# Attention scores of a head pair: one head after the other, or both heads' passes in turn into two PSUM tiles

## The chip, the cores and the metric

The kernel runs on one core of one Trainium2 chip. The metric is device time in microseconds (us) of one execution. Before the change the median of three executions is 1733.63 us (1733.34 to 1735.73).

The core has engines that work side by side and wait for one another through semaphores: TensorE (PE in the profile, with its weight loads as PEld), VectorE (DVE), ScalarE (ACT), GpSimd (POOL) and SyncE (SP), which here issues the weight transfers. Data lie in SBUF, 128 partitions wide. TensorE writes into PSUM, which this kernel uses as eight banks of 128 x 512 fp32 values.

## The reference

A trunk of two layers over 256 latent and 256 context tokens, model width 1024. Layer 0 has a recurrent mixer, layer 1 windowed attention; each stands between two SwiGLU feed-forwards. The change lies in the attention of layer 1 (16 query heads of width 64, 4 key/value heads, blocks of 128 queries):

```python
s_band = jnp.where(valid, jnp.einsum('bqhgd,bkhd->bhgqk', qj, kj).astype(f32), -jnp.inf)
s_ctx = jnp.einsum('bqhgd,bkhd->bhgqk', qj, kc)
p_ctx, p_band = _softmax_with_sink(sink, s_ctx, s_band)
return (jnp.einsum('bhgqk,bkhd->bqhgd', p_ctx.astype(vc.dtype), vc)
        + jnp.einsum('bhgqk,bkhd->bqhgd', p_band.astype(vj.dtype), vj))
```

Each latent query sees 256 context keys and its window of latent keys; with 256 latent tokens that is 512 keys, of which one block of 128 is partly masked. The softmax also has a sink logit for each head.

## The kernel before

Activations are kept transposed (features on partitions, tokens along the row), and every product of the model is made from fp32 values split into a high and a low part in the fp32r type: high x high, high x low, low x high, three matmuls into one PSUM bank (lines 415 to 417; line 444 for the first four blocks of a stage, line 710 in the feed-forwards). SyncE streams the weights in transfers of up to 1 MB; ACT casts the high part (line 259), DVE subtracts for the low part (line 243).

In the attention stage (`odd`) the 16 query heads are packed in eight pairs T = 0 to 7. A pair's query tile `Q[T]` holds one head (half 0) on partitions 0 to 63 and the other (half 1) on 64 to 127; `Q[T][:, 0]` is the high part and `Q[T][:, 1]` the low one. The keys `KH` and `KL` lie the same way, so that each half is a matmul over 64 partitions: `psc` takes 128 queries by 512 keys. With two query blocks t there are four items per T, 32 in all. One item is:

- TensorE: three 64-row passes into one bank `psc` (line 1277 high x high, 1278 high x low, 1279 low x high), and a 128-row bf16 matmul that adds the mask to one block of 128 keys (line 1281, identity `IDB` as weights);
- DVE: the row maximum over `psc` (line 1283) and the scaled, negated bias (line 1284);
- ACT: the exponential into `P` with the row sum (line 1288), put off to the next step;
- four steps later (`LAG`): TensorE turns `P` into `ppt` (line 1298), ACT copies that to `PT` (line 1299).

The loop over n has one item per step. A step stands in this order: work put off by earlier steps (`self.sub`, `self.later`), scores of item n, at the second item of a T the rotary turn of the next pair's queries (`q_rope`: matmul `psw`, line 1224; DVE lines 1229 to 1231; ACT casts the high part, line 1243, DVE makes the low part, line 1244), one quarter of a query projection (`q_piece`, six matmuls of lines 415 to 417, for n up to 24 except n = 8), transposes of item n - 4, and at the first item of a T the values of pair T - 2 (`pov`, line 1313, and the row factors `prs`, line 1319; then lines 1322 to 1325). From n = 31 on the first matmuls of the output projection (line 444) are put between. Each engine works through its instructions in the order in which this code is written. PSUM tiles take the eight banks in turn, and one waits until the bank's earlier tile has been read. `P` has five buffers, `Q` three.

Of the kernel before, what the change touches and what calls it, by code (L numbers as in the profile page):

```python
# [12 lines left out]
AF = mybir.ActivationFunctionType  # L13
ALU = mybir.AluOpType
AX = mybir.AxisListType
# [131 lines left out]
class Trunk:  # L147
# [1054 lines left out]
    def odd(self):  # L1202
        nc, V, S, G, M = self.nc, self.V, self.S, self.G, self.M
        self.narrow()
        with self.tc.tile_pool(name="od", bufs=1) as op:
# [4 lines left out]
            KH = op.tile([128, 2, 512], F32R, name="KH")  # L1210
            KL = op.tile([128, 2, 512], F32R, name="KL")
# [5 lines left out]
            NSK = op.tile([128, 16], F32, name="NSK")  # L1217
            V.tensor_scalar(NSK, SK, -1.0, None, ALU.mult)

            Q, ST, PT, P = {}, {}, {}, {}  # L1220
# [18 lines left out]
            def q_rope(T, stage):  # L1239
                t = raws.pop(T)  # L1240
                rope(t, swap(t), t)
                q = Q[T] = op.tile([128, 2, 256], F32R, tag="q", name="q", bufs=3)
                stage(lambda: S.copy(q[:, 0], t),
                      lambda: V.tensor_tensor(q[:, 1], t, q[:, 0].bitcast(F32), ALU.subtract))

            def k_rope(i):
                x = KF[i][:, 256:512]
                rope(x, swap(x), x)
                self.later(lambda: S.copy(KH[:, i], KF[i]),
                           lambda: V.tensor_tensor(KL[:, i], KF[i], KH[:, i].bitcast(F32), ALU.subtract))  # L1250

            pss = self.split_start("o", 2)
# [3 lines left out]
            for T in range(2):  # L1256
                ps = self.bank()
# [7 lines left out]
            def head_of(T, half):  # L1265
                return (2 * (T // 4) + half) * 4 + T % 4

            def scores(T, half, t):
                g = 2 * (T // 4) + half
                if half == t == 0:  # L1270
                    ST[T] = op.tile([128, 5, 4], F32, tag="st", name="st", bufs=4)
                i = 2 * half + t
                st = ST[T]
                b = slice(64 * half, 64 * half + 64)
                ps = self.bank("psc")
                q = slice(128 * t, 128 * t + 128)
                M.matmul(ps, lhsT=Q[T][b, 0, q], rhs=KH[b, g // 2, :], start=True, stop=False, skip_group_check=True)  # L1277
                M.matmul(ps, lhsT=Q[T][b, 0, q], rhs=KL[b, g // 2, :], start=False, stop=False, skip_group_check=True)  # L1278
                M.matmul(ps, lhsT=Q[T][b, 1, q], rhs=KH[b, g // 2, :], start=False, stop=False, skip_group_check=True)  # L1279
                kt = 3 - t  # L1280
                M.matmul(ps[:, 128 * kt:128 * kt + 128], lhsT=self.IDB, rhs=self.MKB[:, 1 - t], start=False, stop=True, skip_group_check=True)
                hd = head_of(T, half)
                V.tensor_reduce(st[:, 0, i:i + 1], ps, AX.X, ALU.max)
                V.tensor_scalar(st[:, 1, i:i + 1], st[:, 0, i:i + 1], -0.125, NSK[:, hd:hd + 1], ALU.mult, ALU.min)

                def exp():
                    p = P[T, half, t] = op.tile([128, 512], F32, tag="P", name="P", bufs=5)
                    S.activation(p, ps, AF.Exp, scale=0.125, bias=st[:, 1, i:i + 1], accum_out=st[:, 2, i:i + 1])

                self.later(exp)  # L1290

            def transposes(T, half, t):
                if t == 0:
                    PT[T, half] = op.tile([128, 4, 256], F32, tag="PT", name="PT", bufs=4)
                p = P.pop((T, half, t))
                ps = self.bank("ppt")
                for k in range(4):
                    M.transpose(ps[:, 128 * k:128 * k + 128], p[:, 128 * k:128 * k + 128], self.ID)  # L1298
                S.copy(PT[T, half][:, :, 128 * t:128 * t + 128], ps.rearrange("p (k q) -> p k q", k=4))
                if half == t == 1:  # L1300
                    st = ST[T]
                    for x in range(2):
                        hd = head_of(T, x)
                        S.activation(st[:, 3, 2 * x:2 * x + 2], st[:, 1, 2 * x:2 * x + 2], AF.Exp, bias=SK[:, hd:hd + 1])
                    V.tensor_tensor(st[:, 2], st[:, 2], st[:, 3], ALU.add)
                    V.reciprocal(st[:, 4], st[:, 2])

            def values(T):
                ps = self.bank("pov")
                for kt in range(4):  # L1310
                    for half in range(2):
                        g = 2 * (T // 4) + half
                        M.matmul(ps[64 * half:64 * half + 64, 0:256], lhsT=VT[:, kt, 64 * g:64 * g + 64],  # L1313
                                 rhs=PT[T, half][:, kt, :], start=kt == 0, stop=kt == 3, skip_group_check=True)
                pr = self.bank("prs")
                for t in range(2):
                    for half in range(2):
                        i = 2 * half + t
                        M.matmul(pr[64 * half:64 * half + 64, 128 * t:128 * t + 128], lhsT=ST[T][:, 4, i:i + 1].to_broadcast([128, 64]),
                                 rhs=self.ID, start=True, stop=True)  # L1320
                rb = self.tmp("rb")
                S.copy(rb[:, 0:256], pr[:, 0:256])
                self.later(lambda: V.tensor_tensor(rb[:, 256:512], ps[:, 0:256], rb[:, 0:256], ALU.mult),
                           lambda: S.copy(OH[:, T], rb[:, 256:512]),
                           lambda: V.tensor_tensor(OL[:, T], rb[:, 256:512], OH[:, T].bitcast(F32), ALU.subtract))
                PT.pop((T, 0))
                PT.pop((T, 1))
                Q.pop(T)
                ST.pop(T)

            items = [(T, half, t) for T in range(8) for half in range(2) for t in range(2)]
            LAG = 4
            PIECES = {p + (p >= 8): p for p in range(24)}
            EARLY = range(31, 36)
# [2 lines left out]
            def q_piece(T, i):  # L1337
                if i == 0:
                    qp[T] = self.bank()
                wh, wl = self.weight(("oq", T))  # L1340
                for kt in (2 * i, 2 * i + 1):
                    c = slice(128 * kt, 128 * kt + 128)
                    self.mm3(qp[T][:, 0:256], wh[:, c], wl[:, c], self.NH[:, kt, 256:512], self.X[1][kt][:, 256:512], kt == 0, kt == KT - 1)
                if i == 3:
                    q_load(T, qp.pop(T))
                    self.done(("oq", T))

            for n in range(len(items) + LAG + 1):
                T, i = n // 4, n % 4
                self.sub()  # L1350
                if n < len(items):
                    scores(*items[n])
                if i == 1 and T < 7:
                    q_rope(T + 1, self.later)
                if n == 3:
                    k_rope(1)
                if n in PIECES:
                    p = PIECES[n]
                    q_piece(2 + p // 4, p % 4)
                if LAG <= n < len(items) + LAG:  # L1360
                    transposes(*items[n - LAG])
                if i == 0 and T > 1:
                    values(T - 2)
                if n == EARLY[0]:
                    pss = [self.bank() for _ in range(4)]
                    early = self.steps(pss, "oo", [(0, 256)] * 4, src=os)
                if n in EARLY:
                    next(early)
# [5 lines left out]
            for m in range(8):  # L1374
                ps = pss[m] if m < 4 else self.bank()
# [185 lines left out]
```

## Time and profile before

| | us |
|---|---|
| median of three executions | 1733.63 |
| span of the profiled execution, first to last instruction | 1731.2 |
| PE busy | 1719.7 |
| DVE busy | 1145.0 |
| ACT busy | 653.7 |
| score matmuls, lines 1277 to 1281, first to last start | 1418.5 to 1499.8 |

Of the profiled execution the record gives the span and no other time; the three executions that were timed lie 2.1 to 4.5 us above that span. The granted TensorE clock is 0.998 of full speed on average. Times within the profile are counted from the span's first instruction. A matmul's own duration runs from its start until its result is out; since matmuls are pipelined, what one costs TensorE is the distance from one start to the next, which the chain of waits shows.

### The profile page before, as it was taken

The page shows a single profiled execution, that of the slowest core. Times are in us where ns is not written, and L with a number is a line of the kernel's source. Part 1 is how long each engine was busy: PE and PEld are TensorE (multiplying, and loading weights), DVE is VectorE, ACT ScalarE, POOL GpSimd, SP SyncE. Part 2 cuts the span into 40 slices and gives each one's busy share as a digit, 9 for nine tenths or more (in the row PEclk, how much of TensorE's full clock was granted, in tenths as well). Part 3 has the DMA queues.
Part 4 walks back from the last instruction along what each step waited for, and adds up shares of the span by engine and source line. Part 5 has one row for each costly group of instructions (what it writes and reads, how often), then busy time and mean ns, then how long its engine had stood idle before and what let it go on. Part 6 is the DMA issues. An engine that isn't in the chain of part 4 may idle for free.

```text
span 1731.2 us, 23818 instructions
## 1 busy us (share of the span) xinstructions
PE 1719.7 (99%) x9702; PEld 1446.9 (84%) x9702; DVE 1145.0 (66%) x1997; ACT 653.7 (38%) x1083; POOL 24.7 (1%) x29
## 2 busy tenths in 40 slices
PE   9999999999999999999999999999999999999998
PEld 7778778779788898787787897787788897799998
DVE  6876776767878767767765378555543476576665
ACT  4421222235546453212222352222222456654444
POOL 0000000000001100000000000000000000000000
PEclk9999999999999999999999999999999999999999
DMA  9554444541212234445434144435533031165540
GB/s 372 220 192 148 171 174 146 180 158 44 74 49 74 101 143 153 188 146 194 171 130 150 45 162 160 181 146 194 190 142 107 15 116 50 49 228 191 191 155 30
DMA packets 36463, 247.87 MB, mean 143 GB/s; under 512 B 4001, under 2 KB 4257, under 8 KB 8961
## 3 DMA queue, kind: packets, MB, share of 16 engines
q1 hardware_dynamic: 35792, 244.57, 38.7%
q8 instruction: 76, 1.25, 0.3%
q0 software_dynamic: 272, 1.25, 0.2%
q10 hardware_dynamic: 288, 0.52, 0.1%
q14 instruction: 35, 0.28, 0.0%
HBM read 245.28 MB, written 1.05 MB: 142 GB/s over the span
## 4 chain that ended last, share of the span: by engine, by line
PE 97%; DVE 1%; ACT 1%; DMA 0%; issue 0%; SPq 0%; POOLq 0%; ACTq 0%; DVEq 0%
PE bank L415 25%; PE bank L417 25%; PE bank L416 25%; PE bank L710 5%; PE bank L444 4%; PE bank L1126 1%; PE bank L1124 1%; PE bank L1125 1%; PE pva L337 1%; PE pov L1313 1%; PE ppt L1298 1%; PE psc L1277 1%; PE pO L1006 0%; PE psc L1279 0%; PE psc L1278 0%; PE pada L383 0%
## 5 line engine op out<-in xcount | busy, mean ns | idle before, releaser
L415 PE MATMUL bank<-NH,wh 128*128 128x512 f32 (+2 forms) x1416 | 518.6, 366 | 0.0
L417 PE MATMUL bank<-NH,wl 128*128 128x512 f32 (+2 forms) x1416 | 514.4, 363 | 1.2 <-DVE wl L243 1.2
L416 PE MATMUL bank<-NL,wh 128*128 128x512 f32 (+2 forms) x1384 | 498.8, 360 | 0.0
L415 PEld LDWEIGHTS bank<-NH,wh 128*128 128x128 f32 x1416 | 266.2, 188 | 48.8 <-issue 9.0
L417 PEld LDWEIGHTS bank<-NH,wl 128*128 128x128 f32 x1416 | 265.8, 188 | 47.2 <-DVE wl L243 1.7
L416 PEld LDWEIGHTS bank<-NL,wh 128*128 128x128 f32 x1384 | 260.1, 188 | 45.2
L259 ACT CAST wh<-raw 128x1024 fp32r<-128x1024 f32 (+1 forms) x207 | 212.4, 1029 | 153.5 <-PE bank L416 99.8
L415 PE MATMUL bank<-HH,wh 128*128 128x512 f32 (+1 forms) x776 | 269.6, 347 | 0.0
L416 PE MATMUL bank<-HL,wh 128*128 128x512 f32 (+1 forms) x776 | 268.3, 346 | 0.1
L417 PE MATMUL bank<-HH,wl 128*128 128x512 f32 (+1 forms) x776 | 268.2, 346 | 0.0
L243 DVE TENSOR_TENSOR wl<-raw,wh 128x1024 fp32r<-128x1024 f32 (+1 forms) x207 | 247.2, 1198 | 18.7 <-ACT wh L259 18.7
L625 DVE SCALAR_TENSOR_TENSOR H<-bank,mods,H 128x256 f32<-128x256 f32 x192 | 86.7, 481 | 174.1 <-PE bank L417 171.3
L790 ACT CAST HH<-hd 128x512 fp32r<-128x512 f32 (+1 forms) x88 | 49.9, 567 | 320.5 <-DVE hd L789 285.2
L259 ACT CAST wh<-rawx 128x1024 fp32r<-128x1024 f32 (+1 forms) x118 | 119.7, 1016 | 118.2 <-PE bank L416 102.2
L415 PEld LDWEIGHTS bank<-HH,wh 128*128 128x128 f32 x776 | 147.0, 189 | 20.1 <-issue 2.5
L416 PEld LDWEIGHTS bank<-HL,wh 128*128 128x128 f32 x776 | 147.1, 190 | 18.1 <-DVE HL L791 0.3
L417 PEld LDWEIGHTS bank<-HH,wl 128*128 128x128 f32 x776 | 147.0, 189 | 17.9
L322 DVE SCALAR_TENSOR_TENSOR va<-rawx,SC,va 128x512 f32<-128x512 f32 x228 | 159.8, 748 | 1.2
L789 DVE TENSOR_TENSOR hd<-sg,bank 128x512 f32<-128x512 f32 x66 | 45.3, 687 | 168.3 <-PE bank L417 162.8
L243 DVE TENSOR_TENSOR wl<-rawx,wh 128x1024 fp32r<-128x1024 f32 (+1 forms) x118 | 139.1, 1182 | 3.6 <-ACT wh L259 3.6
L322 DVE SCALAR_TENSOR_TENSOR va<-raw,SC,va 128x512 f32<-128x512 f32 x164 | 114.1, 748 | 0.4
L780 ACT ACTIVATE sg<-bank 128x512 f32<-128x512 f32 x66 | 39.5, 598 | 155.1 <-PE bank L417 154.6
(291 smaller groups left out, 1784.2 us busy)
## 6 DMA issues: line engine op xcount, KB each, us to landing
raw<-w SPq DMA_DIRECT2D x123, 1024.0 KB, 4.8
rawx<-w SPq DMA_DIRECT2D x91, 1024.0 KB, 4.8
rawx<-w SPq DMA_DIRECT2D x7, 768.0 KB, 4.2
raw<-w SPq DMA_DIRECT2D x6, 768.0 KB, 4.2
raw<-w SPq DMA_DIRECT2D x3, 896.0 KB, 4.5
H<-xt SPq DMA_DIRECT2D x4, 512.0 KB, 5.2
rawx<-w SPq DMA_DIRECT2D x2, 896.0 KB, 4.5
raw<-w SPq DMA_DIRECT2D x2, 512.0 KB, 10.0
```

Of the source, the lines that this page charges most:

```text
L243: self.V.tensor_tensor(lo[:, :n], src, hi[:, :n].bitcast(F32), ALU.subtract)
L259: self.S.copy(hi[:, :n], src)
L322: V.scalar_tensor_tensor(acc[:, s], src, c, acc[:, s], ALU.mult, ALU.add)
L415: self.M.matmul(ps, lhsT=wh, rhs=xh, start=start, stop=False)
L416: self.M.matmul(ps, lhsT=wh, rhs=xl, start=False, stop=False)
L417: self.M.matmul(ps, lhsT=wl, rhs=xh, start=False, stop=stop)
L444: self.M.matmul(pss[i][:, 0:hi - lo], lhsT=w[wi][:, c:c + 128], rhs=(xh, xl)[xi][kt][:, lo:hi], start=n == b == 0, stop=n == 3 and b == 5)
L625: self.V.scalar_tensor_tensor(self.H[:, m, q], ps[:, c - lo:c - lo + 256], gate[:, m, c // 256:c // 256 + 1], self.H[:, m, q], ALU.mult, A ...
L710: self.M.matmul(pss[i][:, q], lhsT=lhs, rhs=rhs, start=n == b == 0, stop=n == 3 and b == 5)
L780: S.activation(sg, pg, AF.Silu)
L789: V.tensor_tensor(hd, sg, pu, ALU.mult)
L790: S.copy(HH[:, f - fa], hd[:, 0:n])
```

## The change

`scores` now takes a query block t of a pair T and makes both halves: it takes two PSUM tiles at once and issues the high x high pass of half 0 and of half 1, then both high x low passes, then both low x high passes, then both masks. The two maxima and biases follow on DVE, and both exponentials are put off to the next step together. It is called at every other step, and the items run over t before half.

```diff
-            def scores(T, half, t):
-                g = 2 * (T // 4) + half
-                if half == t == 0:
+            def scores(T, t):
+                if t == 0:
                     ST[T] = op.tile([128, 5, 4], F32, tag="st", name="st", bufs=4)
-                i = 2 * half + t
                 st = ST[T]
-                b = slice(64 * half, 64 * half + 64)
-                ps = self.bank("psc")
+                pss = [self.bank("psc") for _ in range(2)]
                 q = slice(128 * t, 128 * t + 128)
-                M.matmul(ps, lhsT=Q[T][b, 0, q], rhs=KH[b, g // 2, :], start=True, stop=False, skip_group_check=True)
-                M.matmul(ps, lhsT=Q[T][b, 0, q], rhs=KL[b, g // 2, :], start=False, stop=False, skip_group_check=True)
-                M.matmul(ps, lhsT=Q[T][b, 1, q], rhs=KH[b, g // 2, :], start=False, stop=False, skip_group_check=True)
                 kt = 3 - t
-                M.matmul(ps[:, 128 * kt:128 * kt + 128], lhsT=self.IDB, rhs=self.MKB[:, 1 - t], start=False, stop=True, skip_group_check=True)
...
+                for n, (x, kk) in enumerate(((0, KH), (0, KL), (1, KH))):
+                    for half, ps in enumerate(pss):
+                        b = slice(64 * half, 64 * half + 64)
+                        M.matmul(ps, lhsT=Q[T][b, x, q], rhs=kk[b, T // 4, :], start=n == 0, stop=False, skip_group_check=True)
+                for ps in pss:
+                    M.matmul(ps[:, 128 * kt:128 * kt + 128], lhsT=self.IDB, rhs=self.MKB[:, 1 - t], start=False, stop=True, skip_group_check=True)
+                for half, ps in enumerate(pss):
+                    i, hd = 2 * half + t, head_of(T, half)
+                    V.tensor_reduce(st[:, 0, i:i + 1], ps, AX.X, ALU.max)
+                    V.tensor_scalar(st[:, 1, i:i + 1], st[:, 0, i:i + 1], -0.125, NSK[:, hd:hd + 1], ALU.mult, ALU.min)
...
+                def exp(half):
+                    i = 2 * half + t
                     p = P[T, half, t] = op.tile([128, 512], F32, tag="P", name="P", bufs=5)
...
+                    S.activation(p, pss[half], AF.Exp, scale=0.125, bias=st[:, 1, i:i + 1], accum_out=st[:, 2, i:i + 1])
-                self.later(exp)
+                self.later(lambda: (exp(0), exp(1)))
...
-            items = [(T, half, t) for T in range(8) for half in range(2) for t in range(2)]
+            items = [(T, half, t) for T in range(8) for t in range(2) for half in range(2)]
...
-                if n < len(items):
-                    scores(*items[n])
+                if n < len(items) and n % 2 == 0:
+                    scores(T, i // 2)
```

The program's order on TensorE shows it, here around one item, with a transpose before it and a query projection behind it. In the rows `psc` is a score tile with its buffer number, `ppt` a transposed block, `IDB` the mask's identity weights and `bank` the query projection. Before:

```order
L1298 MATMUL ppt_11588<-C_70,P_11484 128x128 x4
L1277 MATMUL psc_11601<-KH_10914,q_11533 128x512
L1278 MATMUL psc_11601<-KL_10915,q_11533 128x512
L1279 MATMUL psc_11601<-KH_10914,q_11533 128x512
L1281 LDWEIGHTS IDB_78
L1281 MATMUL psc_11601<-MKB_79,IDB_78 128x128
L415 MATMUL bank_11534<-NH_72,wh_11201 128x256
```

After, at a step of the same kind (line 1278 is now the line of all three passes, 1280 of the mask, 1299 of the transposes):

```order
L1299 MATMUL ppt_11798<-C_70,P_11654 128x128 x4
L1278 MATMUL psc_11806<-KH_10914,q_11663 128x512
L1278 MATMUL psc_11807<-KH_10914,q_11663 128x512
L1278 MATMUL psc_11806<-KL_10915,q_11663 128x512
L1278 MATMUL psc_11807<-KL_10915,q_11663 128x512
L1278 MATMUL psc_11806<-KH_10914,q_11663 128x512
L1278 MATMUL psc_11807<-KH_10914,q_11663 128x512
L1280 LDWEIGHTS IDB_78
L1280 MATMUL psc_11806<-MKB_79,IDB_78 128x128
L1280 LDWEIGHTS IDB_78
L1280 MATMUL psc_11807<-MKB_79,IDB_78 128x128
L415 MATMUL bank_11790<-NH_72,wh_11288 128x256
```

Two items that stood a step apart, each with three passes and a mask, are now one block of six passes in turn between two score tiles, and two masks; the step that follows has no scores.

On DVE, in the second half of a pair T with the low part of the next pair's queries (line 1244) and the low part of an attention output (`OL`). Before:

```order
L1283 TENSOR_REDUCE st_11486<-psc_11551 128x1
L1284 TENSOR_SCALAR st_11486<-st_11486,NSK_10919 128x1
L1325 TENSOR_TENSOR OL_10918<-rb_11515,OH_10917 128x256
L1244 TENSOR_TENSOR q_11533<-qr_11468,q_11533 128x256
L1283 TENSOR_REDUCE st_11486<-psc_11575 128x1
```

After:

```order
L1283 TENSOR_REDUCE st_11486<-psc_11552 128x1
L1284 TENSOR_SCALAR st_11486<-st_11486,NSK_10919 128x1
L1283 TENSOR_REDUCE st_11486<-psc_11553 128x1
L1284 TENSOR_SCALAR st_11486<-st_11486,NSK_10919 128x1
L1326 TENSOR_TENSOR OL_10918<-rb_11522,OH_10917 128x256
L1244 TENSOR_TENSOR q_11535<-qr_11470,q_11535 128x256
```

The second maximum of the block has moved ahead of the low parts of `OL` and `q`.

On ACT, from the last steps of T = 1 to the values of pair 0 (`qr` is the query projection's result, `wh` the cast of the next weights, `rb` the row factors). Before:

```order
L1288 ACTIVATE P,st<-psc,st 128x512
L1237 COPY qr<-bank 128x256
L259 CAST wh<-raw 128x1024
L1299 COPY PT<-ppt 128x4x128
L1304 ACTIVATE st<-st,SM 128x2 x2
L1288 ACTIVATE P,st<-psc,st 128x512
L1299 COPY PT<-ppt 128x4x128
L1322 COPY rb<-prs 128x256
```

After:

```order
L1289 ACTIVATE P,st<-psc,st 128x512 x2
L1237 COPY qr<-bank 128x256
L259 CAST wh<-raw 128x1024
L1300 COPY PT<-ppt 128x4x128
L1305 ACTIVATE st<-st,SM 128x2 x2
L1300 COPY PT<-ppt 128x4x128
L1323 COPY rb<-prs 128x256
```

Both exponentials of a block stand together ahead of the query copy and the cast, and none stands any more between the two copies of `PT`.

More of the change, by code (lines that the diff above doesn't have):

```diff
@@ L1282, in scores @@
[L1282 to L1286, printed above, removed]
+                for n, (x, kk) in enumerate(((0, KH), (0, KL), (1, KH))):
+                    for half, ps in enumerate(pss):
+                        b = slice(64 * half, 64 * half + 64)
+                        M.matmul(ps, lhsT=Q[T][b, x, q], rhs=kk[b, T // 4, :], start=n == 0, stop=False, skip_group_check=True)
@@ L1287, in exp @@
                     p = P[T, half, t] = op.tile([128, 512], F32, tag="P", name="P", bufs=5)
-                    S.activation(p, ps, AF.Exp, scale=0.125, bias=st[:, 1, i:i + 1], accum_out=st[:, 2, i:i + 1])
-                self.later(exp)
+                    S.activation(p, pss[half], AF.Exp, scale=0.125, bias=st[:, 1, i:i + 1], accum_out=st[:, 2, i:i + 1])
+                self.later(lambda: (exp(0), exp(1)))
             def transposes(T, half, t):
```

## The prediction

> **What bounds the kernel now.** I read the page's busy times and its chain of waits first. TensorE works nearly without a break, and the chain that ends last runs through it:
>
> ```profile
> PE 1719.7 (99%) x9702; PEld 1446.9 (84%) x9702; DVE 1145.0 (66%) x1997; ACT 653.7 (38%) x1083; POOL 24.7 (1%) x29
> PE 97%; DVE 1%; ACT 1%; DMA 0%; issue 0%; SPq 0%; POOLq 0%; ACTq 0%; DVEq 0%
> ```
>
> So time that TensorE no longer needs is time gained, as long as the others keep up. How much room they have comes from the table of stretches: the whole attention stage, one head pair with query projections, and the last two pairs without.
>
> ```profile
> core 0: us, PE busy (x) PEld busy (x) DVE busy (x) ACT busy (x) POOL busy (x), PEclk, DMA share, GB/s
> 1410.00:1520.00 110.00, 109.97 (x784) 84.37 (x783) 67.58 (x151) 71.01 (x169) 0.00 (x0) 1.00 0.17 62
> 1475.30:1487.10 11.80, 11.80 (x85) 8.66 (x83) 7.17 (x17) 7.62 (x19) 0.00 (x0) 1.00 0.21 83
> 1487.10:1495.90 8.80, 8.80 (x61) 5.62 (x59) 5.85 (x16) 6.16 (x17) 0.00 (x0) 1.00 0.00 1
> 1495.90:1504.60 8.70, 8.70 (x67) 6.21 (x65) 4.93 (x11) 6.13 (x16) 0.00 (x0) 1.00 0.09 13
> ```
>
> The granted clock is 1.00, the transfers take 0.17 of the DMA engines, and a pair takes 11.80 us because TensorE is busy for 11.80; ACT needs 7.62 of them, DVE 7.17. In the last two pairs the room is smaller, 8.8 against 6.2.
>
> What one item of the scores costs TensorE comes from the chain of waits in order of time (start, length up to the next piece). First one step with a query projection, then one without, where the item stands between two groups of transposes:
>
> ```profile
> 1477.62 0.44 PE ppt L1298 x4
> 1478.05 0.43 PE psc L1277
> 1478.48 0.23 PE psc L1278
> 1478.71 0.24 PE psc L1279
> 1478.95 0.16 PE psc L1281
> 1479.11 0.17 PE bank L415
> 1479.28 0.12 PE bank L416
> ...
> 1484.84 1.88 PE pov L1313 x16
> 1486.72 0.44 PE prs L1319 x8
> ...
> 1488.70 0.44 PE ppt L1298 x4
> 1489.13 0.42 PE psc L1277
> ...
> 1490.19 0.44 PE ppt L1298 x4
> ```
>
> An item takes 1490.19 - 1489.13 = 1.06 us. A pass of 512 columns is 0.23; the first takes 0.20 more, and the mask, a quarter of the columns and so about 0.06, takes 0.16. The weight loads show where these extras lie:
>
> ```profile
> 1444.27 0.46 PEld L1298 LDWEIGHTS ppt<-C,P 128*128 128x128 f32 x4
> 1444.89 0.18 PEld L1277 LDWEIGHTS psc<-KH,q 64*128 64x128 f32 x1 [0.17 <-DVE st L1284]
> 1445.00 0.19 PEld L1278 LDWEIGHTS psc<-KL,q 64*128 64x128 f32 x1
> 1445.24 0.18 PEld L1279 LDWEIGHTS psc<-KH,q 64*128 64x128 f32 x1
> 1445.79 0.10 PEld L1281 LDWEIGHTS <-IDB 128*128 128x128 bf16 x1 [0.36 <-issue]
> ...
> PEld L1281 <- issue: 11.7, 32, 0.4
> PEld psc L1277 <- issue: 3.7, 22, 0.2
> ```
>
> Elsewhere a load runs ahead while the matmul before it streams. On going from 128 rows to 64 (line 1277) loading pauses for 0.17, and on going back (line 1281) for 0.36, in all 32 items, with nothing to wait for. So each item pays one way into the 64-row shape, where the load of 0.11 (1445.00 - 1444.89) is bare too, and one way out. Together that is 0.20 + 0.10 of its 1.06.
>
> **The change part by part.** *The passes.* No row shows two matmuls on different halves of the rows. The nearest are those on different halves of the columns: `pov` and `prs`, whose two heads write partitions 0 to 63 and 64 to 127 in turn. Against them stands `psw` on the whole array, the same 256 fp32 columns (these count as two instructions each):
>
> ```profile
> 1449.40 0.44 PE L1313 MATMUL pov<-PT,VT 128*64 128x256 f32 x2
> L1313 PE MATMUL pov<-PT,VT x128: 378/379/431, 1437.6 to 1513.4; 128*64 128x256 f32 x128
> ...
> 1452.67 0.65 PE L1224 MATMUL psw<-qr,TR 128*128 128x256 f32 x2
> L1224 PE MATMUL psw<-qr,TR x16: 379/408/483, 1415.1 to 1488.3; 128*128 128x256 f32 x16
> ```
>
> Two of `pov` take 0.44 together where one takes up to 0.431, so they start within about 0.01 of each other; two of `psw` take 0.65, and start some 0.27 apart. Sixteen of `pov` in 1.88 make eight pairs of 0.235, about the price of one `psw`. Column halves thus run at the same time in this program. The two row halves of a score block use separate rows, separate weights and separate banks, and I take them to run together likewise. A block is then 0.43 + 0.23 + 0.24 + 0.16 as one item is now, plus the second mask at 0.06 = 1.12, in place of 2 x 1.06 = 2.12. It saves 1.00, and 16 blocks save **16.0 us**.
>
> Bounds. Nothing saved by the overlap would leave the serial case below. Within the overlap, the second half's first load may have to follow the first half's (0.11 more a block, 1.8 in all), and the second mask may cost the full 0.16 of the first (1.6 in all); in the other direction the 0.05 that the first matmul of a projection pays behind an item (0.17 against 0.12) disappears at about 12 steps (0.6). The gain on TensorE is 12.6 to 16.6. I take 16.0, as loads of different halves of `pov` do not queue visibly.
>
> The Trainium skill, TensorE: Matmul & The Clock Gate, "Part 3: Packing small matmuls — row/col tiling", says that matmuls on different row groups run concurrently as well, and gives a speedup of 3.07 for four row tiles of 512 columns; no run here shows it. An estimate from that page's figure: at the same 0.77 of the ideal, two tiles reach 1.54, three pairs of passes take 0.90 instead of 0.70, the 16.0 becomes 12.8, and the forecast would be 3.2 us later.
>
> *The maxima, the exponentials, the order of items.* Their number and size stay. Two maxima now stand back to back on DVE and two exponentials on ACT, and what stood between them comes later. These rows price it (nanoseconds in the first four, us in the others):
>
> ```profile
> L1283 DVE TENSOR_REDUCE st<-psc x32: 659/692/693, 1419.7 to 1500.0; 128x1 f32<-128x512 f32 x32
> L1288 ACT ACTIVATE P<-psc,st x32: 672/692/709, 1422.0 to 1501.3; 128x512 f32<-128x512 f32 x32
> L1288 ACT ACTIVATION_READ_ACCUMULATOR P<-psc,st x32: 193/202/218, 1422.6 to 1501.9; 128x1 f32 x32
> L1299 ACT COPY PT<-ppt x32: 575/586/597, 1429.2 to 1511.0; 128x512 f32<-128x512 f32 x32
> 1444.53 0.21 DVE L1284 TENSOR_SCALAR st<-st,NSK 128x1 f32<-128x1 f32 x1
> 1444.66 0.41 DVE L1325 TENSOR_TENSOR OL<-rb,OH 128x256 fp32r<-128x256 f32 x1
> 1444.99 0.42 DVE L1244 TENSOR_TENSOR q<-qr,q 128x256 fp32r<-128x256 f32 x1
> 1449.07 0.37 ACT L1237 COPY qr<-bank 128x256 f32<-128x256 f32 x1 [0.19 <-PE bank L417]
> 1449.34 1.05 ACT L259 CAST wh<-raw 128x1024 fp32r<-128x1024 f32 x1
> ```
>
> In the middle of the stage TensorE needs 11.80 - 2.00 = 9.80 a pair, still more than ACT's 7.62. The low part of the next queries is the tightest handover. From the second block's masks DVE needs 2 x (0.69 + 0.21) + 0.41 + 0.42 = 2.63. TensorE reaches the third pair of passes, which reads that low part, after two projections (0.17 + 5 x 0.12 = 0.77 each), two groups of transposes (0.44 each) and two pairs of passes (0.66) = 3.08: 0.45 to spare. Three places lack that cover:
> - The last pair's first block (step 28), where no projections are left: 0.88 + 0.66 = 1.54 against 2.63, a wait of 1.1 behind which the masks, transposes and values queue.
> - The values of pair 0 (step 8, the one step that skips its projection). ACT has the exponentials done 2.69 after the masks of step 6, then the query copy 0.37, the cast 1.05 and the `PT` copy 0.59: 4.70. TensorE arrives after 2 x (0.77 + 0.44) + 1.12 + 0.44 = 3.98: 0.7.
> - The last blocks: ACT needs 2 x 0.69 + 2 x 0.59 = 2.56 a block, TensorE 1.12 + 0.88 = 2.00. Three blocks fall back by 1.7, of which the values of pair 4 (1.88 + 0.44) cover part; I take 1.2.
>
> Sum of waits 3.0; between 0, if the overlaps of neighbouring instructions on ACT and DVE cover them, and 5, if each place costs some half more. Behind the stage nothing changes but its start: weights come through the same ring, the DMA share there was 0.17, and a later stretch that began earlier keeps its own length.
>
> Net: 16.0 - 3.0 = **13.0 us**; with both bounds 7.6 to 16.6. The profiled span of 1731.2 would become 1718.2; the median of the timed runs lies 2.4 above that span, and 1733.6 - 13.0 = **1720.6**, own range 1717.0 to 1726.0.
>
> **The rivals.**
> 1. *Row halves don't overlap*, so the change doesn't do what it is made for. Six passes follow one another: 0.20 + 6 x 0.23 + 0.16 + 0.06 = 1.80 a block, 0.32 less than two items, since half of the ways in and out go. 5.1 less about 1.0 for the waits of steps 8 and 28: 1729.5. For it speaks that no row shows such a pair; against it the column halves.
> 2. *The readers set the pace.* Maxima and exponentials of a block end later than TensorE's next work allows, not at three places but in each of the five middle pairs too. Priced at one exponential with its read (0.69 + 0.20 = 0.9) per pair, 4.5 more: 1725.1. Against it speaks ACT's 7.62 in 9.80. The Trainium skill, TensorEngine Tiling (Array Packing), "PSUM Bottleneck", states the rule behind it: tiling speeds up TensorE but not the emptying of PSUM. The trace agrees only for the last two pairs.
> 3. *Slower: each change of half drains the array*, as each change between 64 and 128 rows does now. Then all six passes cost what the first does: 6 x 0.43 + 0.16 + 0.06 = 2.80 a block against 2.12, 16 x 0.68 = 10.9 more: 1744.5. It decides once a change of half costs over 0.32 / 5 = 0.064 without overlap. Against it speak `pov`'s column halves, which alternate sixteen times with no such pause; for it, only that rows are not columns.
>
> **How the numbers follow.** Forecast 0.74, rival 1 0.12, rival 2 0.07, rival 3 0.05, and 0.02 for a loss of another kind. The time is the forecast's, 1720.6. The range from 1717.0 goes up over rival 2 and just over rival 1, to 1730.0; outside lie rival 3, the rest and about a third of rival 1, some 0.13 in all with the low tail. What a measurement of this kernel can tell from no change is about 0.2%, 3.5 us, so that faster begins below 1730.1. Faster: the forecast and rival 2 (0.81) and half of rival 1, 0.86; same: the rest of rival 1 and a little, 0.08; slower 0.06.
>
> **What would show it.** Right: in the changed profile two passes of a block start within 0.02 of each other, a block's rows in the chain sum to about 1.1, and the middle pairs take about 9.8 instead of 11.8; the idle time of weight loads before the mask falls to 16 times. Short waits of TensorE appear before the third pair of passes at step 28 and before the values of pair 0. Rival 1 shows as six starts 0.23 apart, rival 2 as waits on ACT or DVE before `psc` or `pov` in every pair, rival 3 as pauses of the loads inside a block. The forecast falls if the rows of a block sum to over 1.8, or if the stages behind the attention grow by what it loses.

## The result, and the profile after

The changed kernel takes 1722.78 us, median of four executions (1720.98 to 1723.75), against 1734.28 (1733.34 to 1735.73) for the kernel before beside it: a ratio of 0.9928, 95% interval 0.9916 to 0.9940. That is 11.5 us less; 1720.6 was forecast.

The changed profile has a span of 1721.6. TensorE still sets the pace, and its chain still holds nearly all of the span:

```profile
PE 1706.8 (99%) x9702; PEld 1441.0 (84%) x9702; DVE 1143.2 (66%) x1997; ACT 652.8 (38%) x1083; POOL 24.7 (1%) x29
PE 96%; DVE 2%; ACT 1%; DMA 0%; issue 0%; SPq 0%; POOLq 0%; ACTq 0%; DVEq 0%
```

One middle pair, from the start of one pair's values to the next, in the table of stretches: first a pair of the kernel before, then two of the changed kernel.

```profile
1449.47:1461.26 11.79, 11.79 (x85) 8.65 (x86) 7.18 (x18) 7.62 (x20) 0.00 (x0) 1.00 0.25 89
```

```profile
core 0: us, PE busy (x) PEld busy (x) DVE busy (x) ACT busy (x) POOL busy (x), PEclk, DMA share, GB/s
1447.67:1457.56 9.89, 9.89 (x84) 7.78 (x86) 6.97 (x18) 7.51 (x20) 0.00 (x0) 1.00 0.30 106
1457.56:1467.44 9.88, 9.88 (x84) 7.77 (x86) 6.96 (x18) 7.50 (x20) 0.00 (x0) 1.00 0.01 2
```

The stretch is 1.90 shorter, and the busy times of DVE and ACT barely move. The chain of waits of the changed kernel shows the new block of scores:

```profile
1459.43 0.44 PE prs L1320 x8
1459.87 0.63 PE psw L1224 x2
...
1461.21 0.44 PE ppt L1299 x4
1461.65 0.90 PE psc L1278 x6
1462.55 0.22 PE psc L1280 x2
1462.76 0.17 PE bank L415
...
1467.44 1.88 PE pov L1314 x16
```

Six passes take 0.90 and two masks 0.22, together 1.12 where two items took 2.12. How the passes run is seen in the timeline of the changed kernel, loads first, then two rows of matmuls:

```profile
1441.81 0.19 PEld L1278 LDWEIGHTS psc<-KH,q 64*128 64x128 f32 x2 [0.17 <-issue]
1441.92 0.19 PEld L1278 LDWEIGHTS psc<-KL,q 64*128 64x128 f32 x2
1442.16 0.19 PEld L1278 LDWEIGHTS psc<-KH,q 64*128 64x128 f32 x2
1442.70 0.11 PEld L1280 LDWEIGHTS <-IDB 128*128 128x128 bf16 x2 [0.36 <-issue]
...
1441.82 0.50 PE L1278 MATMUL psc<-KH,q 64*128 64x512 f32 x2
1442.15 0.39 PE L1278 MATMUL psc<-KL,q 64*128 64x512 f32 x2
```

Each row holds two instructions and is no longer than one was before (0.50 for the first pass, 0.39 for the second). So both halves load their weights together and stream together. The pause on the way out, 0.36, is met 16 times instead of 32:

```profile
PEld L1280 <- issue: 5.6, 16, 0.4
```

Since the first part of an execution differs from one to the next, I compare kernels from the start of the first score matmul to the span's end as well. These are 1731.2 - 1418.5 = 312.7 before and 1721.6 - 1421.5 = 300.1 after: 12.5 less before rounding. The 3 us between this and the spans' difference of 9.6 lie in the first 25 us, before any changed instruction, as the first start of line 444 shows (before, then after):

```profile
L444 PE MATMUL bank<-NH,wh x80: 277/392/503, 21.8 to 1540.9; 128*128 128x512 f32 x48, 128*128 128x258 f32 x32
```

```profile
L444 PE MATMUL bank<-NH,wh x80: 278/392/505, 24.7 to 1531.3; 128*128 128x512 f32 x48, 128*128 128x258 f32 x32
```

Over the ten profiles of this study that start lies anywhere from 21.8 to 25.6, whatever the kernel; the kernel before happened to have the earliest. The medians below carry some 1 to 2 us that no edit explains (1722.78 and 1724.05 for the same kernel), which is of this size. The second column, one profiled execution for each kernel, gives 300.1 and 300.2 for that kernel and so says more of the edits. Each ratio is to the kernel before as it was timed beside that run (medians 1734.28, 1734.12 or 1734.36).

| kernel | median, us | first score to end, us | ratio to before, 95% interval |
|---|---|---|---|
| before | 1734.28 | 312.7 | |
| changed | 1722.78 | 300.1 | 0.9928 (0.9916 to 0.9940) |
| changed, again | 1724.05 | 300.2 | 0.9937 (0.9924 to 0.9949) |
| same half, two query blocks | 1731.61 | 309.7 | 0.9983 (0.9974 to 0.9993) |
| half after half | 1723.79 | 301.6 | 0.9940 (0.9925 to 0.9954) |
| changed, low part a step earlier | 1726.82 | 304.5 | 0.9954 (0.9939 to 0.9969) |
| before, low part a step earlier | 1735.17 | 312.8 | 1.0004 (0.9995 to 1.0013) |
| changed, low part on GpSimd | 1722.13 | 300.0 | 0.9928 (0.9916 to 0.9941) |
| changed, exponentials a step later | 1720.98 | 298.5 | 0.9923 (0.9910 to 0.9935) |
| changed, both of these | 1719.52 | 298.7 | 0.9916 (0.9902 to 0.9929) |

### The profile page after: what moved, and what is told of

Read it like the earlier page. It is cut to its first block, busy times and chain, and to the rows that moved or that the text cites. A ratio compares the mean times of both kernels' runs of the same rounds, so it can differ in the third digit from the quotient of the medians.

```text
span 1721.6 us, 23813 instructions
## 1 busy us (share of the span) xinstructions
PE 1706.8 (99%) x9702; PEld 1441.0 (84%) x9702; DVE 1143.2 (66%) x1997; ACT 652.8 (38%) x1083; POOL 24.7 (1%) x29
## 4 chain that ended last, share of the span: by engine, by line
PE 96%; DVE 2%; ACT 1%; DMA 0%; issue 0%; SPq 0%; POOLq 0%; ACTq 0%; DVEq 0%
PE bank L415 25%; PE bank L417 25%; PE bank L416 25%; PE bank L710 5%; PE bank L444 4%; PE bank L1126 1%; PE bank L1125 1%; PE bank L1124 1%; PE pva L337 1%; PE pov L1314 1%; PE psc L1278 1%; PE ppt L1299 1%; PE pada L383 0%; DMA H<-xt 0%; PE pO L1006 0%; PE pB L1008 0%
```

## The experiments

Two questions stood: whether the gain comes from row halves that run at the same time or from having half as many changes of shape; and where the time goes that TensorE still waits.

**The same half twice.** The two tiles of a block are the two query blocks of one head, so that the passes keep taking turns between two banks, but all use the same 64 rows:

```diff
-            def scores(T, t):
+            def scores(T, half):
...
+                b = slice(64 * half, 64 * half + 64)
                 for n, (x, kk) in enumerate(((0, KH), (0, KL), (1, KH))):
-                    for half, ps in enumerate(pss):
-                        b = slice(64 * half, 64 * half + 64)
+                    for t, ps in enumerate(pss):
+                        q = slice(128 * t, 128 * t + 128)
                         M.matmul(ps, lhsT=Q[T][b, x, q], rhs=kk[b, T // 4, :], start=n == 0, stop=False, skip_group_check=True)
```

> Blocks of six passes in turn into two score tiles as in the changed kernel, but the two tiles are the two query blocks t of one half, so all six passes use the same 64 rows. The number of ways into and out of the 64-row shape is that of the changed kernel (16 each). Theory (different row halves run at the same time): no overlap is left, passes start 0.23 apart, a block takes 1.80, 0.32 less than two items; 5.1 saved less about 1.0 of waits: near 1730, first score to end about 308.5 against 312.6 before and 300.1 after. Rival (the gain comes from half as many shape changes and from two banks in turn): as the changed kernel, near 1722, 300.1 from the first score to the end.

Measured: 1731.61, and 309.7 from the first score to the end. Its chain of waits has blocks of this length:

```profile
1453.57 1.58 PE psc L1277 x6
1455.16 0.22 PE psc L1280 x2
```

1.58 + 0.22 = 1.80 is the price that was worked out for six passes without overlap. The theory of no overlap held, with a stretch 1.2 longer than its 308.5. Halving the changes of shape, less the waits that come with it, is worth about 3 of the 12.5 (312.7 - 309.7); the other 9.6 (309.7 - 300.1) comes only when the passes use different rows. The middle pairs, where TensorE waits for no other engine, say the same: 11.79 us before, 11.27 with the same half, 9.89 with both halves. Without the way in (0.20), six passes take 1.38 on the same rows and 0.70 on different ones, a ratio of 1.97. The Trainium skill, TensorE: Matmul & The Clock Gate, "Part 3: Packing small matmuls — row/col tiling", has 3.07 for four row tiles, from which the prediction drew 1.54 for two as an estimate; the measurement is nearer to the full 2.

**Half after half.** The block keeps its place, but the program issues three passes of half 0 and then three of half 1:

```diff
-                for n, (x, kk) in enumerate(((0, KH), (0, KL), (1, KH))):
-                    for half, ps in enumerate(pss):
-                        b = slice(64 * half, 64 * half + 64)
+                for half, ps in enumerate(pss):
+                    b = slice(64 * half, 64 * half + 64)
+                    for n, (x, kk) in enumerate(((0, KH), (0, KL), (1, KH))):
```

> The changed kernel with the six passes of a block in another order: three of half 0, then three of half 1. Theory (a pass overlaps only with a neighbour in program order on the other rows, issue is in order): only the third pass of half 0 and the first of half 1 run together, five slots of 0.23: 0.20 + 5 x 0.23 + 0.22 = 1.57 a block, 0.55 saved, 8.8 in all less 1.5 of waits: near 1727, first score to end about 305. Rival (the engine takes passes of the other half ahead by itself): as the changed kernel, 1722. Rival (no overlap at all): 1730.

Measured: 1723.79, and 301.6, within 1.5 of the changed kernel: my theory of issue in order fell and the first rival held. In the middle pairs, blocks of two lengths take turns in its chain of waits; the timeline shows the slower kind:

```profile
1449.53 0.91 PE psc L1278 x6
...
1453.00 1.11 PE psc L1278 x6
```

```profile
1442.83 0.71 PE L1278 MATMUL psc<-KH,q 64*128 64x512 f32 x2
1443.17 0.60 PE L1278 MATMUL psc<-KL,q 64*128 64x512 f32 x2
1443.40 0.61 PE L1278 MATMUL psc<-KH,q 64*128 64x512 f32 x2
```

The program's order is KH, KL, KH for half 0, then the same for half 1. On the chip two KH passes start before any KL, 0.2 apart in this block and together in the other kind. So the first pass of half 1 started ahead of the second of half 0: TensorE took an instruction for the free row half past those that waited for the busy one. What stands ahead of the prediction, that each engine works in the order of the code, therefore does not hold for TensorE within a block. The Trainium skill, TensorE: Matmul & The Clock Gate, "Part 3: Packing small matmuls — row/col tiling", says that matmuls start and end strictly in program order; here the measurement decides against it.

The slower kind is the first block of a pair, whose third pass reads the new low part of the queries. First the low part and the first load of half 1 in the block above, then a window around step 28, where the low part is latest:

```profile
1442.56 0.42 DVE L1244 TENSOR_TENSOR q<-qr,q 128x256 fp32r<-128x256 f32 x1
1443.04 0.18 PEld L1278 LDWEIGHTS psc<-KH,q 64*128 64x128 f32 x1
```

```profile
1481.02 0.49 PE L1278 MATMUL psc<-KH,q 64*128 64x512 f32 x1
1481.36 0.39 PE L1278 MATMUL psc<-KL,q 64*128 64x512 f32 x1
1482.23 0.42 DVE L1244 TENSOR_TENSOR q<-qr,q 128x256 fp32r<-128x256 f32 x1
1482.70 0.50 PE L1278 MATMUL psc<-KH,q 64*128 64x512 f32 x2 [0.95 <-DVE q L1244]
```

At step 28 the third pass of half 0 waits for DVE, and the first pass of half 1, which needs nothing of DVE, starts only with it, 1.68 behind the block's first. So the program does stand half after half, and TensorE passed over instructions that waited for rows, but not over one that waited for another engine. That is the price of the written order: 0.2 in the first block of a middle pair, more where the low part comes later.

**The waits.** In the changed kernel, from the first score on, TensorE's loads wait for other engines four times for longer than 0.2. Three of these stand in rows of its timeline, two at step 8 and, behind the break, one at step 28, each with the instructions that end last ahead of it; the fourth is 0.34 before the values of step 32:

```profile
1435.54 0.19 PEld L1278 LDWEIGHTS psc<-KH,q 64*128 64x128 f32 x2 [0.37 <-DVE q L1244]
1435.87 0.36 ACT L1237 COPY qr<-bank 128x256 f32<-128x256 f32 x1
1436.12 1.06 ACT L259 CAST wh<-raw 128x1024 fp32r<-128x1024 f32 x1
1437.07 0.59 ACT L1300 COPY PT<-ppt 128x512 f32<-128x512 f32 x1
1437.71 0.41 PEld L1314 LDWEIGHTS pov<-PT,VT 128*64 128x64 f32 x6 [0.90 <-ACT PT L1300]
...
1483.38 0.21 DVE L1284 TENSOR_SCALAR st<-st,NSK 128x1 f32<-128x1 f32 x1
1483.51 0.42 DVE L1326 TENSOR_TENSOR OL<-rb,OH 128x256 fp32r<-128x256 f32 x1
1483.84 0.42 DVE L1244 TENSOR_TENSOR q<-qr,q 128x256 fp32r<-128x256 f32 x1
1484.31 0.19 PEld L1278 LDWEIGHTS psc<-KH,q 64*128 64x128 f32 x2 [1.38 <-DVE q L1244]
```

The first edit moves the low part ahead of the maxima, one step earlier:

```diff
-                stage(lambda: S.copy(q[:, 0], t),
-                      lambda: V.tensor_tensor(q[:, 1], t, q[:, 0].bitcast(F32), ALU.subtract))
+                def split():
+                    S.copy(q[:, 0], t)
+                    V.tensor_tensor(q[:, 1], t, q[:, 0].bitcast(F32), ALU.subtract)
+
+                stage(split)
```

> The changed kernel with the low part of the next queries made one step earlier, right behind its cast, so that on DVE it stands ahead of the second block's two maxima. Theory (the waits of 0.37 at step 8 and 1.38 at step 28 come from that low part standing behind two maxima): both go, about 1.5 less than the changed kernel from the first score to the end, 298.6, time near 1721. Rival (DVE or ACT is short there anyhow and the wait moves to the next reader): no change against 300.1.

Measured: 1726.82, and 304.5, slower than the change by 4.4 in that stretch. In the list of this kernel's waits (who for whom, total, times, longest):

```profile
DVE q L1245 <- ACT q L1244: 7.5, 8, 1.4
...
PEld pov L1317 <- ACT PT L1303: 4.6, 3, 2.6
```

The wait for the low part is gone, but DVE now stands up to 1.4 waiting for the cast, with the maxima behind it; so the exponentials and the copies behind them come later, and the values wait up to 2.6. The rival held: the wait moved to the next reader, and grew. The same edit in the kernel before costs nothing:

> The kernel before with the same single move of the low part as in the run with the changed kernel. Theory: before the change nothing waited for it, so no change: 1734, 312.6 from the first score to the end. Rival (the low part was late before too): about 1 less.

Measured: 1735.17, ratio 1.0004 (0.9995 to 1.0013), and 312.8. In neither profile of the kernel before does a load of TensorE wait for the low part or for the `PT` copy; its longer score items leave room for both orders.

The next edit leaves the place and changes the engine, so that the low part stands behind nothing of DVE's:

```diff
-                      lambda: V.tensor_tensor(q[:, 1], t, q[:, 0].bitcast(F32), ALU.subtract))
+                      lambda: G.tensor_tensor(q[:, 1], t, q[:, 0].bitcast(F32), ALU.subtract))
```

> The changed kernel with the low part of the next queries subtracted on GpSimd instead of DVE, in its place in the program. It then stands behind nothing. Theory (waits at steps 8 and 28 come from its place behind two maxima, and behind them wait the exponentials and copies): the waits of TensorE for it (0.37 and 1.38) go, but the values of steps 8 and 28 then wait for the PT copy, some 1.1 and 0.8; about 0.8 less than the changed kernel, 299.3. Rival (GpSimd is slower than the wait, over 2 us for 256 columns): more than 300.1.

Measured: 1722.13, and 300.0: nothing that can be told from the change. The line's own view and the waits of TensorE's loads in this kernel:

```profile
L1244 POOL TENSOR_TENSOR q<-qr,q x8: 731/732/1815, 1419.4 to 1481.8; 128x256 fp32r<-128x256 f32 x8
...
PEld pov L1314 <- ACT PT L1300: 1.6, 3, 0.9
PEld psc L1278 <- POOL q L1244: 1.1, 2, 0.6
```

The wait at step 28 fell from 1.38 to 0.43, but the values behind it then waited 0.35; and GpSimd's first subtraction took 1.8 instead of 0.73 and left the loads of the very first block idle for 0.65. What it gained at two places it lost at two others.

The third edit takes the exponentials out of the way of the copy that the values need:

```diff
-                self.later(lambda: (exp(0), exp(1)))
+                self.later(lambda: None, lambda: (exp(0), exp(1)))
```

> The changed kernel with the two exponentials of a block put off by one more step, so that on ACT the PT copy that the values need stands ahead of them. Theory (the waits of the values at steps 8 and 32, 0.90 and 0.34, come from that copy standing behind two exponentials): both go, about 1.2 to 1.6 less than the changed kernel, 298.5 to 298.9; the wait at step 28 for the low part stays. Rival (banks held one step longer stop the next block's scores): a new wait before psc in every pair, over 300.1.

Measured: 1720.98, and 298.5, 1.7 less than the change's 300.2 beside it. The waits of the values at steps 8 and 32 are gone: from the first values of pair 0 to those of pair 1 it takes 9.88 instead of 10.97, from pair 6 to pair 7 9.55 instead of 10.08, together 1.6. Holding the score banks a step longer cost nothing in the middle pairs, which stay at 9.89. What is left of TensorE's loads waiting for `psc` stands at steps 8 and 28:

```profile
PEld psc L1278 <- DVE q L1244: 1.1, 2, 0.7
PEld psc L1278 <- ACT q L1243: 0.9, 1, 0.9
```

The second of these is new: at step 28 the cast of the high part stands behind the exponentials now. The last kernel has both edits:

> Both of the two edits before: low part on GpSimd and exponentials a step later. Theory: all four waits of TensorE go but for about 0.8 at step 28; 2.4 less than the changed kernel, 297.7, near 1721. Rival (ACT or DVE are short and the wait only moves): within 0.5 of 300.1.

Measured: 1719.52, and 298.7. Only part of the theory held: the exponentials' edit gives its 1.5 to 1.7, GpSimd adds nothing (0.65 lost at the first block, 0.52 + 0.86 still waited at step 28). The kernel with the exponentials a step later is the better one by its stretch and the one with both edits by its median; the difference between them is not settled. Both lie below the changed kernel measured beside them:

> The changed kernel once more, beside the next three on the same chip: 1722 to 1724, 300.1 from the first score to the end.

Measured: 1724.05, and 300.2.

## Why the prediction was right

The forecast was 1720.6, a gain of 13.0, with 0.86 for faster; 1722.78 and 11.5 were measured, 12.5 of gain in the part of the program that the change can reach. Step by step:

- **A block at 1.12.** It measured 0.90 + 0.22 = 1.12. The choice to read the row halves by the column halves of `pov` was right, and the same-half run shows that the overlap and not the rarer change of shape carries three quarters of the gain.
- **Sixteen blocks, 16.0.** The middle pairs give 1.90 each and not 2.00. I had priced the ways into and out of the 64-row shape, but not that `psw`, which used to follow a score item, now follows `prs`, which uses half the columns. In the chain it takes 0.63 (the row 1459.87 above) instead of 0.49, and the loads pause before it as they had not done before; first the kernel before, then the changed one:

```profile
1452.84 0.49 PE psw L1224 x2
```

```profile
PEld psw L1224 <- issue: 0.9, 5, 0.2
```

The 0.14 is a change of shape that had been counted with the scores and stayed. Against it stands the 0.05 that a projection costs more behind an item: 2.00 + 0.05 - 0.14 = 1.91. In the whole stage `prs` is followed so six times (five times by `psw`, once by transposes), and six projections less stand behind scores: 16.0 - 6 x 0.14 + 6 x 0.05 = 15.5. This unpriced term of 0.5 is the difference between the 13.0 of the forecast and the 12.5 measured.

- **The waits, 3.0.** What is left, 15.5 - 12.5 = 3.0, is the sum that was forecast, but by luck: its parts were off and their errors cancelled. From one pair's values to the next, step 8 cost 10.97 - 9.89 = 1.08 where 0.7 was expected, and step 32, for the last blocks, 10.08 - 9.55 = 0.53 where 1.2 was. Step 28 cost about 1.2 where 1.1 was: from the values of pair 4 to those of pair 5 it took 8.79 before and takes 8.15, 0.64 saved of 2.00 - 0.14. A wait of 0.37 for the low part at step 8 came on top, which I had not seen; in time it is 0.1. In its rows DVE makes a low part of the keys there (line 1250, 0.68) ahead of the queries' turn; that this is what makes it late was not tested. The idle times of the loads (0.90, 0.34, 1.38, 0.37) sum to 2.99 too, but place by place they are not what the wait costs.
- **The bounds.** "7.6 to 16.6" does not follow from the terms: 16.0 less 5 and less 0 is 11.0 to 16.0. The measured gain lies within both.
- **What lies outside.** The stages behind the attention kept their length, as assumed: from the values of pair 7 to the end it is 219.4 in both kernels. The remaining 1.0 between 12.5 and the medians' 11.5 is of the size by which the start of an execution varies; that it comes from there was seen for the profiled executions (21.8 against 24.7), not for the others.

Of the rivals, the one without overlap gave 1729.5; built as a kernel with the same rows twice it took 1731.6. Readers that set the pace in every pair would have shown in the middle pairs, where TensorE waits for no other engine. The slower rival, in which each change of half costs what the way into the shape does, is excluded by the two loads that start together and by a block of 1.12 where it gave 2.80.

## What to carry to other kernels

In this kernel two matmuls over 64 partitions each, on different halves of the rows, into separate banks and with nothing of another shape between them, cost what one does (three pairs in 0.70 against 1.38). Matmuls into one bank were not tried. The changes of shape around them are worth counting too, at about 0.3 us a round trip here, and part of that (0.14) moved to the neighbour when a block was taken out. When the bound engine gets faster by a sixth, look for the places where its cover was thinnest: work put late on a second engine by a pairing (maxima, exponentials) shows first where filler work ends. Moving such work earlier can cost more than it saves, if it must wait itself in a queue that others stand in; putting the work that nobody waits for behind the work that somebody waits for was what helped.

## What had not been expected of the hardware

TensorE started a pass for the free row half ahead of earlier passes for the busy one, so that the program's order within a block of six hardly mattered in the middle pairs: 0.91 or 1.11 for the passes of a block, where issue in order would have given 1.57 - 0.22 = 1.35. It did not do so past a pass that waited for DVE (1.68 at step 28). How far ahead it looks was not measured. And GpSimd's subtraction of 128 x 256 values took 0.73 us, but 1.8 the first time.
